# Gated DeltaNet and MoBA trunk on one core: the transposed 32x32 blocks of a merge from one VectorE transposition, not from TensorE products

## The chip, the core and the metric

The kernel runs on one core of a Trainium2 chip. The metric is the device time of one execution in microseconds (us); lower is better. Before the change three runs took 305.55, 305.79 and 303.6 us, the median is 305.55 us. One more execution was profiled. It took 301.56 us, of which 299.7 us lie between the first and the last instruction of the program.

## The reference, cut to what matters

A sequence of 256 positions of width 1024 goes through a gated-DeltaNet layer and then through a MoBA attention layer; each is followed by a layer norm over a weighted residual. All is float32. The change lies in the first layer, in the solution of small unit lower triangular systems:

```
def gated_delta_rule_chunked(q, k, v, g, beta):
    ...
    lower = jnp.where(strict, jnp.einsum('nbhid,nbhjd->nbhij', k_beta, k) * decay, 0.0)
    a_mat = jnp.eye(C, dtype=jnp.float32) + lower
    w = lax.linalg.triangular_solve(a_mat, k_beta * jnp.exp(gc)[..., None],
                                    left_side=True, lower=True, unit_diagonal=True)
    u = lax.linalg.triangular_solve(a_mat, v * beta[..., None],
                                    left_side=True, lower=True, unit_diagonal=True)
```

Around it stand projections of the input (q, k, v, z), a causal convolution of four taps, a read-out with an RMS norm and a gate, an output projection, and in the second layer the projections k, q, v, z, one 256-wide causal softmax attention for each of 8 heads, and an output projection.

## The kernel before, in words

Weights arrive as raw tiles of 128x1024, in the order in which they are used. ScalarE rounds each to a high part (`hi`), VectorE subtracts to get the low part (`lo`), and TensorE makes every projection as three products, high by high, high by low and low by high. A raw tile's place is free for the next load when its `lo` is written. Every instruction is recorded through small helpers, so that a profile gives nearly all of them one line (L220), and groups are told apart by tile names.

The kernel works with chunks of 128 positions, so that each of the 8 heads has two triangular 128x128 matrices, 16 in all. They are inverted in two groups of four heads, 8 matrices each, by `inverse(grp)`. VectorE or GpSimd inverts the 16x16 diagonal blocks. Then the blocks are merged: 16 to 32, 32 to 64, 64 to 128. The tile `TR` of a group holds its result `RR`, a working copy `TC` with two halves, half 0 with the inverses of the diagonal blocks and half 1 with the transposes of these, and `T64`. In the merge of 16 to 32, which the change touches, four 32x32 blocks lie in the four quarters of the partitions and 8 matrices side by side:

- `ps_x`: products of the matrix blocks (`ME`) by half 0 of `TC`; VectorE copies a part of the result under a mask into `XI` (COPY_PREDICATED).
- `ps_y`: products of half 1 of `TC` and `XI` in both orders, which give the 32x32 inverses and their transposes; ScalarE copies both from PSUM back into `TC` at once, 512 columns.
- VectorE copies diagonal blocks of `TC` into `RR` and `T64` (six copies, TR<-TR), and the merge of 32 to 64 begins: `ps_x5`, a ScalarE copy to `X`, `ps_y5`, then 64 to 128 with `ps_x6` and `ps_y6`. (The profile leaves the 5 and 6 out: x of 32x32 with 32 records and y<-TR,X are the second merge, 64x64 the third.)

A product of float32 operands shows as two records on TensorE in the trace, one of the rounded type or a transposition as one.

The group's result goes to `solve(grp)`: products `ps_s`, and for each chunk a read-out, `read_out`: products `ps_o`, ScalarE squares (`jk`), VectorE `rs`, a power on GpSimd, VectorE `og` (four instructions), TensorE transposition `ps_og`, ScalarE `o`, VectorE `o`. The first products of the output projection (`ps_y<-hi,o`) need both read-outs of group 0.

What sets the order of the instructions on each engine is a planner that runs while the kernel is written down. Projections are the spine of TensorE's queue; after each step of the spine the planner looks at a list of chains (the convolutions, `inverse`, `solve`, `read_out`, layer norms) by rank, and issues the next step of each whose operands it holds to be there by its own table of costs. The splits of weights into `hi` and `lo` are issued in the same way. So another instruction in one chain can move steps of the others in all queues. When the spine needs something that is not there, the planner lets TensorE's time run on until it is.

Of the kernel before, what the change touches and what calls it, by code (L numbers as in the profile page):

```python
# [307 lines left out]
def body(ctx, tc, x, xt, cst_in, w0, wp, a_ln_g, a_ln_b, b_ln_g, b_ln_b, out):  # L308
    ctx.enter_context(tc.manual_schedule())
    nc = Clock(tc.nc)  # L310
# [3 lines left out]
    def rot(pool, shape, dtype, tag, name, bufs):  # L314
        assert tag in ("raw", "hi", "lo") or free(tag)(), (tag, name)
        t = pool.tile(shape, dtype, tag=tag, name=name, bufs=bufs)
        nc.rotate(rings.setdefault(tag, [bufs]), t, bufs)
        return t

    def free(tag, n=1):  # L320

        def test():
            ring = rings.get(tag, [9])
            last = len(ring) - ring[0]
            return all(ring[i] in ended for i in range(max(1, last), max(1, last + n)))
        return test

    def end(*tiles):
        ended.update(getattr(t, "tensor", t).name for t in tiles)
# [13 lines left out]
    def bank(shape, name):  # L343
        return rot(psB, [P] + shape, F32, "b", name, NB)

    def acc(name):
        ring = rings.get("a", [9])
        old = ring[-NA] if len(ring) > NA else None
        pipe.wait(lambda: free("a")() and (old is None or nc.last[old] + 150 <= pipe.now() + 50))
        return rot(psA, [P, 512], F32, "a", name, NA)  # L350
# [168 lines left out]
    blocks = [slice(32 * b, 32 * b + 32) for b in range(4)]  # L519

    XI = [cst.tile([P, 8, 32], F32, name=f"XI{g}") for g in range(2)]
# [146 lines left out]
    def gs_head(h):  # L668
# [41 lines left out]
        if n_md[h // 4] == 4:  # L710
            pipe.add(inverse(h // 4), R_INV)
# [8 lines left out]
    def inverse(grp):  # L720
# [9 lines left out]
        TC = T[:, 1024:1536].rearrange("p (w q c) -> p w q c", w=2, q=8)  # L730
# [35 lines left out]
        ps = bank([8, 32], "ps_x")  # L766
# [4 lines left out]
        nc.vector.copy_predicated(XI[grp], m32.to_broadcast([P, 8, 32]), ps)  # L771
        end(ps)
        yield "t", [XI[grp], free("b")]
        ps = bank([2, 8, 32], "ps_y")
        for q in range(8):
            for b in blocks:
                nc.tensor.matmul(ps[b, 0, q, :], TC[b, 1, q, :], XI[grp][b, q, :], start=True, stop=True)
            for b in blocks:
                nc.tensor.matmul(ps[b, 1, q, :], XI[grp][b, q, :], TC[b, 1, q, :], start=True, stop=True)
        yield "a", [ps]  # L780
        nc.scalar.copy(TC, ps)
        end(ps)
        yield "t", [TC, free("b")]
        for b in blocks:
# [4 lines left out]
        ps = bank([8, 32], "ps_x5")  # L789
# [9 lines left out]
        ps = bank([2, 8, 32], "ps_y5")  # L799
# [12 lines left out]
        ps = bank([8, 64], "ps_x6")  # L812
# [7 lines left out]
        ps = bank([8, 64], "ps_y6")  # L820
# [205 lines left out]
    ps_y = {}  # L1026
# [186 lines left out]
    ps_y = {}  # L1213
# [14 lines left out]
    ps_y = [acc("ps_y2") for _ in range(2)]  # L1228
# [5 lines left out]
    ps_y = [acc("ps_y2"), acc("ps_y2")[:, 0:256], acc("ps_y2")[:, 0:256]]  # L1234
# [23 lines left out]
```

## Time and profile before

| what | value |
|---|---|
| median of three runs | 305.55 us (303.6 to 305.79) |
| the profiled execution, its span | 301.56 us, 299.7 us |
| TensorE products busy | 289.6 us, 97% of the span |
| VectorE busy | 210.8 us, 70% |
| ScalarE busy | 161.5 us, 54% |
| DMA, mean over the span | 165 GB/s |
| chain that ended last | TensorE 92%, no visible cause ("issue") 4%, VectorE 1%, ScalarE 1% |

The chain that ended last follows the work back from the last instruction to whatever released each step. Products are pipelined in TensorE, so the durations of single products overlap; what counts is the distance from start to start, or the length of a stretch of the chain. The merge of group 0 that the change touches runs from 99.6 to 107 us after the span's start, the one of group 1 from 126.5 to 136 us.

### The profile page before, as it was taken

To read this page: it belongs to the slowest core of one execution; us is meant where nothing else is said; L and a number is where in the kernel's file an instruction comes from. 1 tells how busy PE (TensorE), PEld (TensorE's weight loads), DVE (VectorE), ACT (ScalarE), POOL (GpSimd) and SP (SyncE) were. 2 spreads that over 40 slices of the span, in tenths; PEclk is the share of its full clock that TensorE was granted. 3 is DMA by queue.
4 is the path that set the end of the run, shared out by engine and by line. 5 is a ranking of instruction groups with operands and counts; after the bars stand their busy time and mean duration, and the time that the engine had idled before them with its cause. 6 is when DMAs were issued, how large, how long until landed. Compare 5 with 4: busy or idle time off the path is not lost.

```text
span 299.7 us, 6567 instructions
## 1 busy us (share of the span) xinstructions
PE 289.6 (97%) x2598; PEld 267.7 (89%) x2598; DVE 210.8 (70%) x477; ACT 161.5 (54%) x329; POOL 51.1 (17%) x92
## 2 busy tenths in 40 slices
PE   8999999999999999989999999999999999999990
PEld 7899998999999989978987888999999999998890
DVE  0799389999999586678339993865655655762545
ACT  2689986535776552845533525775555558561000
POOL 8003211348856100110020010000000000000101
PEclk9999999999999999999999999999999999999997
DMA  7996425569576702424449065785444447400012
GB/s 226 375 333 206 142 71 176 178 192 309 172 275 161 260 24 32 124 97 138 150 165 363 31 198 160 266 311 188 143 138 144 148 143 271 142 0 2 0 70 71
DMA packets 19934, 49.43 MB, mean 165 GB/s; under 512 B 6304, under 2 KB 7968, under 8 KB 19904
## 3 DMA queue, kind: packets, MB, share of 16 engines
q1 hardware_dynamic: 18592, 46.73, 47.8%
q0 software_dynamic: 448, 1.18, 1.4%
q10 hardware_dynamic: 864, 1.11, 1.1%
q8 instruction: 20, 0.33, 0.4%
q14 instruction: 10, 0.08, 0.1%
HBM read 46.65 MB, written 2.36 MB: 164 GB/s over the span
## 4 chain that ended last, share of the span: by engine, by line
PE 92%; issue 4%; DVE 1%; ACT 1%; POOL 0%; POOLq 0%; DVEq 0%; ACTq 0%
PE ps_kq L220 15%; PE ps_bkq L220 15%; PE ps_y L220 13%; PE ps_z L220 8%; PE ps_v L220 8%; PE ps_bv L220 7%; PE ps_bz L220 7%; PE ps_g L220 4%; PE ps_o L220 2%; PE ps_ot L220 2%; PE ps_sc L220 2%; PE ps_s L220 1%; PE ps_warm L220 1%; PE ps_x L220 1%; PE ps_gb L220 1%
## 5 line engine op out<-in xcount | busy, mean ns | idle before, releaser
L220 DVE TENSOR_TENSOR lo<-raw,hi 128x1024 fp32r<-128x1024 f32 (+1 forms) x79 | 95.5, 1217 | 10.4 <-ACT hi L220 10.0
L220 ACT CAST hi<-raw 128x1024 fp32r<-128x1024 f32 (+1 forms) x79 | 80.3, 1037 | 8.9 <-DMA raw<-in_wp_dram 4.3
L220 PE MATMUL ps_y<-hi,o 128*128 128x512 f32 (+1 forms) x144 | 43.1, 373 | 0.0
L220 PE MATMUL ps_bkq<-x1h,hi 128*128 128x256 f32 x128 | 37.9, 296 | 0.0
L220 PE MATMUL ps_kq<-xh,hi 128*128 128x256 f32 x128 | 36.9, 288 | 0.0
L220 PE MATMUL ps_kq<-xl,hi 128*128 128x256 f32 x128 | 35.9, 280 | 0.0
L220 PE MATMUL ps_kq<-xh,lo 128*128 128x256 f32 x128 | 35.9, 280 | 0.0
L220 PE MATMUL ps_bkq<-x1l,hi 128*128 128x256 f32 x128 | 35.5, 277 | 0.0
L220 PE MATMUL ps_bkq<-x1h,lo 128*128 128x256 f32 x128 | 35.5, 277 | 0.0
L220 PEld LDWEIGHTS ps_y<-hi,o 128*128 128x128 f32 x144 | 26.1, 189 | 4.3
L220 POOL TENSOR_TENSOR mv<-mv,nhalf 128x1 f32<-128x1 f32 x4 | 3.8, 951 | 133.3 <-DVE mv L220 133.3
L220 PE MATMUL ps_y<-lo,o 128*128 128x512 f32 (+1 forms) x72 | 26.3, 365 | 0.0
L220 DVE SCALAR_TENSOR_TENSOR cv<-ps_kq,cst_sb,cv 128x255 f32<-128x255 f32 (+2 forms) x48 | 21.6, 471 | 4.0 <-ACT cv L220 3.8
L220 PEld LDWEIGHTS ps_bkq<-x1l,hi 128*128 128x128 f32 x128 | 24.1, 188 | 0.2
L220 PEld LDWEIGHTS ps_kq<-xh,lo 128*128 128x128 f32 x128 | 24.3, 190 | 0.0
L220 PEld LDWEIGHTS ps_bkq<-x1h,hi 128*128 128x128 f32 x128 | 24.1, 188 | 0.2
L220 PEld LDWEIGHTS ps_kq<-xh,hi 128*128 128x128 f32 x128 | 24.2, 189 | 0.0
L220 PEld LDWEIGHTS ps_kq<-xl,hi 128*128 128x128 f32 x128 | 24.1, 188 | 0.0
L220 PEld LDWEIGHTS ps_bkq<-x1h,lo 128*128 128x128 f32 x128 | 24.1, 188 | 0.0
L220 PE MATMUL ps_v<-xh,hi 128*128 128x256 f32 x64 | 18.7, 292 | 0.0
L220 PE MATMUL ps_v<-xl,hi 128*128 128x256 f32 x64 | 17.9, 280 | 0.2 <-issue 0.2
L220 PE MATMUL ps_bz<-x1h,hi 128*128 128x256 f32 x64 | 18.1, 282 | 0.0
(177 smaller groups left out, 678.1 us busy)
## 6 DMA issues: line engine op xcount, KB each, us to landing
raw<-in_wp_dram SPq DMA_DIRECT2D x77, 512.0 KB, 4.0
md<-ME POOLq DMA_DIRECT2D x8, 128.0 KB, 2.3
late<-in_x_dram SPq DMA_DIRECT2D x1, 1024.0 KB, 5.0
zraw<-in_w_dram ACTq DMA_DIRECT2D x4, 136.0 KB, 4.3
zraw<-in_w_dram ACTq DMA_DIRECT2D x2, 272.0 KB, 5.0
x_sb<-in_xt_dram SPq DMA_DIRECT2D x4, 128.0 KB, 4.0
x_sb<-in_xt_dram SPq DMA_DIRECT2D x2, 256.0 KB, 4.9
raw<-in_wp_dram SPq DMA_DIRECT2D x2, 256.0 KB, 4.4
```

Source lines behind the costliest of these rows:

```text
L220: r = f(*args, **kw)
```

## The change: what it does, and the diff

The products of `ps_y` that gave the transposed results are left out, 32 for each group, 64 in all. `ps_y` has 256 columns instead of 512. ScalarE copies them into half 0 of `TC`. A single VectorE instruction reads the same PSUM tile, transposes each 32x32 block by itself, and writes half 1 of `TC`.

```diff
@@ -771,14 +771,13 @@
         nc.vector.copy_predicated(XI[grp], m32.to_broadcast([P, 8, 32]), ps)
         end(ps)
         yield "t", [XI[grp], free("b")]
-        ps = bank([2, 8, 32], "ps_y")
+        ps = bank([8, 32], "ps_y")
         for q in range(8):
             for b in blocks:
-                nc.tensor.matmul(ps[b, 0, q, :], TC[b, 1, q, :], XI[grp][b, q, :], start=True, stop=True)
-            for b in blocks:
-                nc.tensor.matmul(ps[b, 1, q, :], XI[grp][b, q, :], TC[b, 1, q, :], start=True, stop=True)
+                nc.tensor.matmul(ps[b, q, :], TC[b, 1, q, :], XI[grp][b, q, :], start=True, stop=True)
         yield "a", [ps]
-        nc.scalar.copy(TC, ps)
+        nc.scalar.copy(TC[:, 0], ps)
+        nc.vector.transpose(TC[:, 1].rearrange("p q c -> p (q c)"), ps.rearrange("p q c -> p (q c)"))
         end(ps)
         yield "t", [TC, free("b")]
         for b in blocks:
```

The planner then moves other steps. Up to `ps_y` of group 0 the queues are the same. The largest move is around the merge of group 1 (its tiles are TR_1361 and XI_149) and the read-outs of group 0. On VectorE, before, from the second `rs` of group 0 on:

```order
L220 SCALAR_TENSOR_TENSOR rs<-sso,eq 128x4
L220 COPY_PREDICATED XI_149<-m_145,ps_x 128x256
L220 SCALAR_TENSOR_TENSOR cv<-ps_v,cst_sb,cv 128x255
L220 TENSOR_TENSOR lo_1707<-raw_1394,hi_1706 128x1024
L220 SCALAR_TENSOR_TENSOR og<-ps_o,rs,zs 128x128 x4
L220 SCALAR_TENSOR_TENSOR cv<-ps_v,cst_sb,cv 128x254
L220 COPY TR_1361<-TR_1361 32x8x32 x6
L220 SCALAR_TENSOR_TENSOR o_1772<-ps_og,nnw,o_1772 128x4x128
L220 COPY TR_1361<-ps_y_2083 32x8x32 x2
```

And in the changed kernel, from the masked copy on:

```order
L220 COPY_PREDICATED XI_149<-m_145,ps_x 128x256
L220 SCALAR_TENSOR_TENSOR cv<-ps_v,cst_sb,cv 128x253
L220 TENSOR_TENSOR lo_1830<-raw_1413,hi_1829 128x1024
L220 SCALAR_TENSOR_TENSOR o_1742<-ps_og,nnw,o_1742 128x4x128
L220 STREAM_TRANSPOSE TR_1361<-ps_y 128x256
L220 SCALAR_TENSOR_TENSOR rs<-sso,eq 128x4
L220 TENSOR_TENSOR lo_1923<-raw_1772,hi_1922 128x1024
L220 COPY TR_1361<-TR_1361 32x8x32 x6
L220 SCALAR_TENSOR_TENSOR og<-ps_o,rs,zs 128x128 x4
L220 COPY TR_1361<-ps_y_2037 32x8x32 x2
L220 TENSOR_TENSOR lo_2030<-raw_1811,hi_2029 128x1024
L220 SCALAR_TENSOR_TENSOR o_1742<-ps_og,nnw,o_1742 128x4x128
```

The second read-out (`rs`, `og`, the last `o`) has moved behind the masked copy and the transposition, the six copies stand ahead of `og` instead of behind it, and two more `lo` stand ahead of the last `o`.

On TensorE, before, where group 1's merge begins:

```order
L220 MATMUL ps_og<-ident,og 128x128 x4
L220 MATMUL ps_o<-Z,ME 128x128 x8
L220 MATMUL ps_x<-TR_1361,ME 32x32 x32
L220 MATMUL ps_vt<-ident,cv 128x128 x2
L220 MATMUL ps_z<-hi_1319,xh 128x256
L220 MATMUL ps_z<-lo_1320,xh 128x256
L220 MATMUL ps_z<-hi_1319,xl 128x256
```

And in the changed kernel:

```order
L220 MATMUL ps_x<-TR_1361,ME 32x32 x32
L220 MATMUL ps_og<-ident,og 128x128 x4
L220 MATMUL ps_z<-hi_1319,xh 128x256
L220 MATMUL ps_z<-lo_1320,xh 128x256
L220 MATMUL ps_z<-hi_1319,xl 128x256
L220 MATMUL ps_o<-Z,ME 128x128 x8
L220 MATMUL ps_y<-XI_149,TR_1361 32x32 x32
```

The products `ps_o` of the second read-out, and the transposition `ps_og` of the first, now come after `ps_x` of the merge; 36 products of `ps_z` stand between the end of `ps_v` and `ps_x`, where there were 21.

On TensorE, before, up to the first product of the output projection:

```order
L220 MATMUL ps_y_2083<-TR_1361,X_2072 32x32 x2
L220 MATMUL ps_z<-hi_1319,xh 128x256
L220 MATMUL ps_z<-lo_1320,xh 128x256
L220 MATMUL ps_z<-hi_1319,xl 128x256
L220 MATMUL ps_z<-hi_1319,xh 128x256
L220 MATMUL ps_z<-lo_1320,xh 128x256
L220 MATMUL ps_z<-hi_1319,xl 128x256
L220 MATMUL ps_y<-hi_1373,o_1772 128x512
```

And in the changed kernel:

```order
L220 MATMUL ps_y_2037<-X_2022,TR_1361 32x32
L220 MATMUL ps_y_2037<-TR_1361,X_2022 32x32 x2
L220 MATMUL ps_og<-ident,og 128x128 x4
L220 MATMUL ps_x_2079<-TR_1361,ME 64x64 x8
L220 MATMUL ps_y<-hi_1373,o_1742 128x512
L220 MATMUL ps_y<-lo_1374,o_1742 128x512
```

The last `ps_z` now stands ahead of `ps_y5`, three products after `ps_x5`; the second `ps_og` and `ps_x6` stand ahead of the first product of the output projection, where 6 products of `ps_z` stood.

## Rows read from the trace of the kernel before

**Rows 1.** The page: busy us, share of the span, instructions, by engine.
```profile
PE 289.6 (97%) x2598; PEld 267.7 (89%) x2598; DVE 210.8 (70%) x477; ACT 161.5 (54%) x329; POOL 51.1 (17%) x92
```
**Rows 2.** The page: the chain that ended last, by engine.
```profile
PE 92%; issue 4%; DVE 1%; ACT 1%; POOL 0%; POOLq 0%; DVEq 0%; ACTq 0%
```
**Rows 3.** Waits of TensorE products: total us, times, longest.
```profile
PE ps_y L220 <- issue: 1.2, 2, 0.9
PE ps_warm L220 <- DVE ones L220: 1.1, 1, 1.1
PE ps_vt L220 <- ACT cv L220: 0.2, 1, 0.2
PE ps_v L220 <- issue: 0.2, 1, 0.2
```
**Rows 4.** Chain in order of time: start, length, work, records.
```profile
105.33 0.22 issue
...
124.73 1.80 PE ps_o L220 x16
...
126.62 1.15 ACT jk L220 x8
...
129.26 0.90 issue
...
134.37 0.33 issue
...
136.70 1.07 PE ps_x L220 x16
```
**Rows 5.** Busy us and records of each engine in stretches of TensorE's queue.
```profile
101.52:102.73 1.21, 1.21 (x129) 1.17 (x128) 1.00 (x1) 0.69 (x1) 0.00 (x0) 1.00 0.33 125
...
130.15:134.35 4.20, 4.20 (x128) 3.76 (x128) 2.79 (x11) 2.00 (x4) 0.00 (x0) 1.00 0.39 131
```
**Rows 6.** DMA queues: packets, MB.
```profile
q8 instruction: 20, 0.33, 0.4%
```
**Rows 7.** Timeline of TensorE: start, us from first start to last end, records.
```profile
126.45 0.75 PE L220 MATMUL ps_x<-TR,ME 32*32 32x32 f32 x64
127.14 0.44 PE L220 MATMUL ps_vt<-ident,cv 128*128 128x128 f32 x2
127.33 0.36 PE L220 MATMUL ps_z<-hi,xh 128*128 128x256 f32 x1
127.53 0.28 PE L220 MATMUL ps_z<-lo,xh 128*128 128x256 f32 x1
127.65 0.28 PE L220 MATMUL ps_z<-hi,xl 128*128 128x256 f32 x1
...
131.96 0.69 PE L220 MATMUL ps_x<-TR,ME 32*32 32x32 f32 x32
132.58 0.66 PE L220 MATMUL ps_og<-ident,og 128*128 128x128 f32 x4
132.99 0.36 PE L220 MATMUL ps_z<-hi,xh 128*128 128x256 f32 x1
...
135.85 0.39 PE L220 MATMUL ps_y<-hi,o 128*128 128x512 f32 x1
```
**Rows 8.** Timeline of VectorE, the same columns, idle time before.
```profile
127.80 0.16 DVE L220 SCALAR_TENSOR_TENSOR rs<-sso,eq 128x4 f32<-128x4 f32 x1 [1.19 <-ACT jk L220]
127.88 0.44 DVE L220 COPY_PREDICATED XI<-m,ps_x 128x256 f32<-128x256 uint8 x1
128.21 0.47 DVE L220 SCALAR_TENSOR_TENSOR cv<-ps_v,cst_sb,cv 128x255 f32<-128x255 f32 x1
128.60 1.21 DVE L220 TENSOR_TENSOR lo<-raw,hi 128x1024 fp32r<-128x1024 f32 x1
129.73 1.12 DVE L220 SCALAR_TENSOR_TENSOR og<-ps_o,rs,zs 128x128 f32<-128x128 f32 x4
130.77 0.47 DVE L220 SCALAR_TENSOR_TENSOR cv<-ps_v,cst_sb,cv 128x254 f32<-128x254 f32 x1
131.48 1.62 DVE L220 COPY TR<-TR 32x256 f32<-32x256 f32 x6 [0.24 <-ACT TR L220]
134.20 0.75 DVE L220 SCALAR_TENSOR_TENSOR o<-ps_og,nnw,o 128x512 fp32r<-128x512 f32 x1 [1.10 <-ACT o L220]
135.15 0.87 DVE L220 COPY TR<-ps_y 32x256 f32<-32x256 f32 x2 [0.20 <-PE ps_y L220]
```
**Rows 9.** VectorE groups by shape: busy us, mean ns.
```profile
L220 DVE TENSOR_TENSOR lo<-raw,hi 128x1024 fp32r<-128x1024 f32 x77 | 94.2, 1230 | 10.2 <-ACT hi L220 9.7
...
L220 DVE COPY late<-ps_ot 128x256 f32<-128x256 f32 x8 | 3.4, 424 | 7.2 <-PE ps_ot L220 7.2
...
L220 DVE COPY TR<-TR 32x256 f32<-32x256 f32 x12 | 3.1, 281 | 0.4 <-ACT TR L220 0.2
```
**Rows 10.** Timeline of ScalarE: copies out of the merges.
```profile
102.89 0.59 ACT L220 COPY TR<-ps_y 128x512 f32<-128x512 f32 x1 [0.69 <-issue]
...
108.41 0.36 ACT L220 COPY TR<-ps_y 32x256 f32<-32x256 f32 x1 [1.51 <-DVE TR L220]
...
132.70 0.75 ACT L220 COPY X<-ps_x 32x256 f32<-32x256 f32 x2 [1.25 <-PE ps_x L220]
```

## The prediction

> **What bounds the kernel now.** First the page's busy shares: TensorE has 97% of the span, VectorE 70%, ScalarE 54% [rows 1]. Since busy products overlap, the chain that ended last comes next: 92% of it is TensorE [rows 2]. Then its waits: after the start, products waited four times, 0.2 us for ScalarE and 1.45 us in three gaps with no visible cause [rows 3, 4]. So a microsecond taken from TensorE's queue is a microsecond of the time, as long as nothing new makes that queue wait. All three gaps lie in the stretch with the small products of the merges.
>
> The gaps have a pattern. From the restart after the gap of 129.26 (at 130.15) to the next gap TensorE ran exactly 128 products and 128 weight loads, 256 instructions [rows 5]. A DMA queue for instructions moved 20 packets, 0.33 MB [rows 6]; 2598 products and as many loads are 20.3 times 256 [rows 1]. I read this as code arriving in blocks of 256 instructions, and TensorE running out of it where 128 products pass fast. The Trainium skill says otherwise in part (Runtime: NRT & Kernel Launch, Instruction fetch mechanics): it gives the same blocks of 256, but holds that fetching them is mostly hidden. By that rule the gaps have another cause and nothing done to the number of products removes them; the rows agree on the block and speak against the hiding.
>
> **The work that goes.** `ps_y` of group 0 has 64 products, 128 records, and took 1.21 us from start to the product behind it [rows 5]. Half of it goes: 0.61 us, and 0.61 us again in group 1, together 1.22 us on the engine that bounds.
>
> ScalarE's copy shrinks from 512 columns, 0.59 us, to 256, which I take at 0.36 us, a copy of as many columns [rows 10]. The profile shows no transposition on VectorE. The row nearest to it copies the same 128x256 float32 from PSUM to SBUF: 0.42 us [rows 9], which I take. Ends of the range: 0.28 us, a 256-column copy within SBUF, and 1.23 us, an instruction of four times the columns [rows 9], should eight blocks need several passes; no row makes it likelier than the plain copy.
>
> **Group 0.** Nothing waits for these 0.42 us: the products that read half 1 are `ps_y5`, and between stand 21 `ps_v`, which I take at the 0.12 us of a `ps_z` (127.53 to 127.65 [rows 7]), and `ps_x5` at 0.63 us (131.96 to 132.58 [rows 7]), 3.1 us. So 0.61 us is gained. The gap of 0.22 us at 105.33 should go too. Its block now holds 19 records of `ps_y`, 29 `ps_v`, `ps_x5` and `ps_y5`, some 4.9 us, while the block of 130.15 had its code after 4.20 us and a gap of 0.33 us [rows 4, 5]. TensorE is 0.83 us early after it.
>
> **Group 1: where it is given back.** I follow the new order with the old durations, start to start.
>
> TensorE before began `ps_x` of group 1 at 126.45 [rows 7]. In the new order `ps_og` (0.41 us, from 132.58 to 132.99 [rows 7]) and `ps_o` (1.80 us [rows 4]) come behind it instead, and 15 products of `ps_z` at 0.12 us, 1.8 us, and one pair `ps_vt`, 0.2 us [rows 7], come ahead. 126.45 - 0.83 - 2.21 + 2.0 = 125.4. Then `ps_x` 0.69 to 126.1, `ps_og` to 126.5, three `ps_z` to 126.85, `ps_o` to 128.65, `ps_y` 0.61 to 129.26.
>
> VectorE takes the masked copy at 126.2, then by the distances of [rows 8]: copy 0.33, cv 0.39, `lo` 1.13, `o` 0.75, to 128.8. The transposition has to wait for `ps_y`, to 129.36, and ends at 129.8. `rs` waits for the squares, 1.15 us behind `ps_o` [rows 4]: it is done at 130.0. From there VectorE has no gap: `lo` 1.13, six copies 1.62, `og` 1.04, two copies 0.87, `lo` 1.13, `o` 0.75. The sum is 6.54 us, so the last `o` is there at 136.5 and the output projection can start at 136.6.
>
> TensorE meanwhile has too little to do: six `ps_z` 0.9, `ps_vt` 0.2, `ps_x5` 0.63, three `ps_z`, to 131.5. The copies to `X` take 0.75 us after `ps_x5` [rows 10], so `ps_y5` runs from 132.0 to 132.65 (0.5 us idle, where six `ps_z` and `ps_og` covered it before). `og` is written at 133.8, so TensorE waits 1.2 us for it, then 0.5 us for `T64` and 0.75 us for `o`. About 2.9 us idle in all, where there were gaps of 0.90 and 0.33 us [rows 4]. The block of code that begins with this `ps_y` ends within `ps_y5`; a gap there as long as the longest, 0.90 us, would be over before `og` is written, so I count none on top.
>
> Before, the output projection started at 135.85 [rows 7], but with `ps_x6` (1.07 us [rows 4]) and a pair `ps_vt` (0.2) still to do, which now are done by then. Like for like that is 137.1. So the change comes out at 136.6 - 137.1 = -0.5 us: of 0.83 + 0.61 us and two gaps, together 2.67 us, some 2.2 us are given back as waits for VectorE. Behind this point the queue has the same products, `lo` is two tiles ahead of what it was, and TensorE had no wait before; I expect none.
>
> **The sum.** 301.56 - 0.5 = 301.1 us against the profiled execution. The median of the runs stands 4.0 us higher than that execution; taken off the median it is 305.0 us.
>
> **The rivals.**
>
> The whole gain arrives. The planner's move costs nothing, because VectorE reaches the last `o` in time (`og` overlaps more than I count, or `ps_z` covers the waits). Then 1.22 us of products and 1.45 us of gaps go: 302.9 us. For it: the planner found this order by its own costs, and before the change its order left only one short wait on ScalarE in the whole kernel [rows 3]. Against it: VectorE's queue from the transposition on, as counted. Chance 0.2.
>
> The products go and the gaps stay. A block of code is then as late as before, wherever it ends. Only 1.22 us are gained: 304.3 us. This is what the hiding in the Trainium skill's page on the runtime would leave, since the gaps would not come from code. Chance 0.1.
>
> Slower than before. VectorE becomes the bound of this stretch by more than I count. From the transposition to the last `o` it has no gap, so what the transposition takes beyond 0.42 us goes one for one to the start of the output projection. The point from which it decides is 0.42 + 0.5 = 0.9 us. At the upper bound of 1.23 us the projection starts 0.8 us later, which is 0.3 us slower than before, 305.85 us; a `lo` more ahead of it (1.13 us), held up by its weights, makes it 307.0 us. For it: 70% of VectorE is busy, and in this stretch all of it. Against it: a plain copy of that shape takes 0.42 us. Chance 0.15.
>
> That the change does not do what it says can be left aside: the new order has 32 products of `ps_y` in each group instead of 64, and one transposition each.
>
> **The numbers.** The forecast, 305.0 us, has 0.55, with -1.2 to +0.5 us around it for my hand count of waits. All cases lie between 302.9 and 307.0 us. The three runs shown differ by 2.2 us, and the profiled execution lies below all of them, so a median may fall half a microsecond beyond the lower end: 302.4 to 307.0 us. About 1%, 3 us, is what a measurement of this kernel can tell from no change. Only the whole gain, -0.9%, comes near that: faster by more than 1% gets 0.09, mostly a part of that rival's 0.2. Slower by more than 1% gets 0.05, since even the bounds of the third rival together stay at half of it. Within 1%: 0.86.
>
> **What would show it.** In the profile after: `ps_y` of the first merge with 64 records in about 0.61 us, twice; a transposition of about 0.4 us; no gap of "issue" at 105 us; the waits of TensorE between 131 and 137 us with VectorE's `og`, `TR` and `o` as what ended them, some 2.9 us in sum instead of 1.2; the first product of the output projection near 136.6 us. If those waits are missing, the first rival is right. If the gaps with no cause are as long as before, the second. If the transposition takes over 0.9 us, the third. I am wrong altogether if the queue behind 140 us shows waits that were not there.

## The result, and the profile after

The changed kernel takes 305.65 us (median of 20 runs, 304.32 to 307.29), the kernel before, on the same chips, 303.5 us (20 runs, 301.6 to 306.31). The ratio is 1.008, with a 95% interval of 1.0061 to 1.010: about 2.4 us slower. (Here and below, a run over 1.5% above the fastest of its kernel is left out of a ratio, so that a ratio is not always the quotient of the medians.) The forecast was a gain of 0.5 us. The sign was wrong. That the time lies only 0.65 us above the forecast of 305.0 us is luck: the forecast was counted from the first three runs of the kernel before, whose median of 305.55 us stands 2 us above that of all 20. The profiled execution took 305.25 us, 303.2 of them span, where before it was 301.56 and 299.7.

The page of the changed kernel: busy us by engine, the granted clock of TensorE in 40 slices, the instruction queue, the chain by engine.

```profile
PE 293.1 (97%) x2470; PEld 270.2 (89%) x2470; DVE 211.5 (70%) x479; ACT 161.5 (53%) x329; POOL 52.6 (17%) x92
...
PEclk9999999999999999995999999999999999999998
...
q8 instruction: 19, 0.31, 0.4%
...
PE 88%; issue 3%; DVE 3%; DMA 2%; ACT 2%; POOL 0%; POOLq 0%; DVEq 0%
```

TensorE has 128 products and 128 weight loads fewer on record and is busy 3.5 us *longer* [rows 1]. The 5 in the row of the clock is the first reason; another, in the second layer, comes at the end. Its waits, as in [rows 3]: the gaps of 1.45 us with no visible cause are gone, and one wait for VectorE has come.

```profile
PE ps_og L220 <- DVE og L220: 1.2, 1, 1.2
PE ps_warm L220 <- DVE ones L220: 1.1, 1, 1.1
PE ps_vt L220 <- ACT cv L220: 0.2, 1, 0.2
```

The merge of group 0 ran with no gap, as forecast. The chain there (start, length, work), where `ps_y` took 1.21 us before [rows 5]:

```profile
102.31 0.68 PE ps_y L220 x50
102.99 1.24 PE ps_v L220 x9
104.24 0.62 PE ps_x L220 x32
```

VectorE from the last step ahead of the transposition to the last `o`, to be held against [rows 8]:

```profile
128.55 0.74 DVE L220 SCALAR_TENSOR_TENSOR o<-ps_og,nnw,o 128x512 fp32r<-128x512 f32 x1
131.21 0.45 DVE L220 STREAM_TRANSPOSE TR<-ps_y 128x256 f32<-128x256 f32 x1 [1.92 <-ACT TR L220]
131.58 0.12 DVE L220 SCALAR_TENSOR_TENSOR rs<-sso,eq 128x4 f32<-128x4 f32 x1
131.62 1.21 DVE L220 TENSOR_TENSOR lo<-raw,hi 128x1024 fp32r<-128x1024 f32 x1
132.75 1.58 DVE L220 COPY TR<-TR 32x256 f32<-32x256 f32 x6
134.37 1.13 DVE L220 SCALAR_TENSOR_TENSOR og<-ps_o,rs,zs 128x128 f32<-128x128 f32 x4
...
138.41 0.75 DVE L220 SCALAR_TENSOR_TENSOR o<-ps_og,nnw,o 128x512 fp32r<-128x512 f32 x1 [0.76 <-ACT o L220]
```

The transposition takes 0.45 us, but VectorE stood still for 1.92 us ahead of it, and not for `ps_y`: it waited for ScalarE's copy out of the same `ps_y`. ScalarE's queue shows what that copy stood behind, a convolution step and the squares:

```profile
130.23 0.29 ACT L220 ACTIVATE jk<-ps_o 128x128 f32<-128x128 f32 x1
...
130.48 0.43 ACT L220 ACTIVATE cv<-cv 128x256 f32<-128x256 f32 x1
130.79 0.39 ACT L220 COPY TR<-ps_y 128x256 f32<-128x256 f32 x1
```

TensorE behind it, beside [rows 7]:

```profile
134.78 1.10 PE L220 MATMUL ps_og<-ident,og 128*128 128x128 f32 x4 [1.19 <-DVE og L220]
136.00 1.55 PE L220 MATMUL ps_x<-TR,ME 64*64 64x64 f32 x16
137.48 0.79 PE L220 MATMUL ps_y<-hi,o 128*128 128x512 f32 x1
```

The first product of the output projection starts at 137.48, before the last `o` is begun at 138.41: it needs the other read-out's `o`, so the wait for the last `o` that I had counted does not exist.

Now two stretches of 2 us after another (stretch, us, then busy us and records of TensorE, weight loads, VectorE, ScalarE, GpSimd, then granted clock, DMA share, GB/s), first of the kernel before, then of the changed one.

```profile
132.00:134.00 2.00, 2.00 (x54) 1.83 (x56) 1.04 (x4) 1.25 (x3) 0.00 (x0) 1.00 0.32 125
134.00:136.00 2.00, 1.67 (x55) 1.52 (x53) 1.57 (x3) 0.16 (x1) 0.00 (x0) 1.00 0.03 8
136.00:138.00 2.00, 2.00 (x21) 1.53 (x20) 1.97 (x4) 1.88 (x4) 0.00 (x0) 1.00 0.00 0
```

```profile
132.00:134.00 2.00, 1.45 (x53) 1.09 (x51) 1.97 (x6) 1.93 (x5) 1.78 (x1) 1.00 0.24 27
134.00:136.00 2.00, 1.10 (x5) 0.56 (x5) 1.89 (x8) 0.19 (x1) 0.00 (x0) 1.00 0.66 229
136.00:138.00 2.00, 2.00 (x17) 1.86 (x18) 1.62 (x2) 1.51 (x3) 0.00 (x0) 0.63 0.04 14
138.00:140.00 2.00, 2.00 (x12) 1.27 (x11) 1.59 (x2) 0.95 (x2) 0.00 (x0) 0.50 0.61 219
```

TensorE lacks 1.45 us of work between 132 and 136 us, and then its granted clock falls to 0.50, that is from 2.4 to 1.2 GHz, from 136.5 to 143.35 us. A queue full of products that runs 6.83 us at half speed loses up to 3.4 us. Before, the clock is 1.00 through all of this.

The bill, by matching TensorE's products of the two profiles one by one: where both queues are still alike, at 100 us, the changed kernel is 0.72 us late, a difference at the start. At 160 us, from where both queues are alike to the end, it is 2.3 us late. So between them the change cost 1.6 us. A last 1.1 us come after 255 us, where each of the last 250 products takes about 4.5 ns longer; that is taken up at the end. The clock's part in this is not the whole 3.4 us: the experiment with idle products below prices it at 1.9 us, so that all the rest of the change *gained* 0.3 us.

### The profile page after: what moved, and what is told of

Its sections match the earlier page's. It is cut to its first block, busy times and chain, and to the rows that moved or that the text cites. A ratio compares the mean times of both kernels' runs of the same rounds, so it can differ in the third digit from the quotient of the medians.

```text
span 303.2 us, 6322 instructions
## 1 busy us (share of the span) xinstructions
PE 293.1 (97%) x2470; PEld 270.2 (89%) x2470; DVE 211.5 (70%) x479; ACT 161.5 (53%) x329; POOL 52.6 (17%) x92
## 4 chain that ended last, share of the span: by engine, by line
PE 88%; issue 3%; DVE 3%; DMA 2%; ACT 2%; POOL 0%; POOLq 0%; DVEq 0%
PE ps_kq L220 15%; PE ps_bkq L220 15%; PE ps_y L220 13%; PE ps_v L220 8%; PE ps_bz L220 7%; PE ps_bv L220 7%; PE ps_z L220 7%; PE ps_g L220 4%; DMA raw<-in_wp_dram 2%; PE ps_ot L220 2%; PE ps_sc L220 2%; PE ps_s L220 1%; PE ps_warm L220 1%; PE ps_x L220 1%; PE ps_gb L220 1%
## 5 line engine op out<-in xcount | busy, mean ns | idle before, releaser
L220 PE MATMUL ps_y<-hi,o 128*128 128x512 f32 (+1 forms) x144 | 44.5, 384 | 0.0
L220 PEld LDWEIGHTS ps_y<-hi,o 128*128 128x128 f32 x144 | 26.8, 194 | 4.9
L220 PE MATMUL ps_y<-lo,o 128*128 128x512 f32 (+1 forms) x72 | 27.2, 378 | 0.0
L220 PE MATMUL ps_bz<-x1h,lo 128*128 128x256 f32 x64 | 17.9, 280 | 0.0
```

The source lines that it names most:

```text
L220: r = f(*args, **kw)
```

## The experiments

**My theory** was that the transposition itself is worth its 2.7 us, and that the new order, with a transposition that waits for ScalarE, leaves TensorE without work and takes its clock. **Rivals**: the transposition costs what it gains; the clock is a by-product that costs nothing; the order alone is to blame.

**The change with the old order.** The planner is told the costs of the 32 products that are gone and of the longer copy; all queues keep the old order. (The helper's line is L238 there, and the new instructions have lines of their own.)

```diff
+        nc.as_before(ps, TC, XI[grp])       # books 32 products on TensorE
         yield "a", [ps]
-        nc.scalar.copy(TC[:, 0], ps)
-        nc.vector.transpose(TC[:, 1]..., ps...)
+        tc.nc.scalar.copy(TC[:, 0], ps)     # issued past the planner
+        tc.nc.vector.transpose(TC[:, 1]..., ps...)
+        nc.copied_as_before(ps, TC)         # books the copy of 512 columns
```

> The change with the order of the kernel before: the planner is told the old costs, so that the queues hold the old order, with 32 products of ps_y in each group left out and one transposition put in. Theory (the new order is what costs, by TensorE's waits and the fall of its clock after them): faster than before by 1.2 to 2.7 us, ratio 0.991 to 0.996, the granted clock at 1.00 between 130 and 145 us. Rival (the transposition itself costs, by VectorE's time and its wait for ScalarE's copy): slower than before as the changed kernel is, ratio 1.005 to 1.010.

Measured: 300.28 us, ratio 0.9898 (0.986 to 0.9936). The theory holds, with a little more gain than its bracket had, and the first rival falls: the same instructions in the old order gain 3.1 us. Its one profiled execution shows that the clock can fall here too. There `ps_y5` of group 0 waited for a transposition that stood behind VectorE steps whose DMA was late; the clock fell behind that wait too (0.50 for 10.24 us from 108.5), and that execution took 304.65 us:

```profile
PE ps_y L238 <- DVE TR L799: 1.5, 1, 1.5
```

**The new order with the old products.** The kernel before, all 64 products and the copy of 512 columns, with the planner's bookings of the changed kernel.

```diff
-                nc.tensor.matmul(ps[b, 1, q, :], XI[grp][b, q, :], TC[b, 1, q, :], ...)
+                tc.nc.tensor.matmul(ps[b, 1, q, :], XI[grp][b, q, :], TC[b, 1, q, :], ...)
-        nc.scalar.copy(TC, ps)
+        tc.nc.scalar.copy(TC, ps)
+        nc.as_changed("Activation", ps, TC[:, 0], 80 + 0.833 * 256)
+        nc.as_changed("DVE", ps, TC[:, 1], 68 + 1.042 * 256)
```

> The kernel before with the order of the changed one: all 64 products of ps_y and the 512-column copy stay, no transposition, but the planner is told the costs of the change. Theory (the order costs): slower than before by the 2.4 us that the changed kernel lost and about 1 us for the products that it saved, ratio 1.008 to 1.013, with waits for VectorE's og and TR between 131 and 137 us and the clock at 0.5 behind them. Rival (the transposition costs): ratio 0.998 to 1.002.

Measured: 304.63 us, 1.0031 (0.9998 to 1.0065). A miss. The order alone costs 0.3%, if anything. Nine of its twelve runs had a mean clock of 0.986 and more; in the profiled one, with 0.985, it fell (0.50 for 6.83 us from 138.3). Its 64 extra products take 1.2 us of TensorE's queue, and nothing waits for a transposition. So the order by itself is not the whole loss.

**Idle products in the hole.** The changed kernel with nine 128x128 products that nobody reads, five ahead of the second `ps_og` and four ahead of `ps_x6`.

```diff
+        for _ in range(0 if grp == 0 else 4):            # ahead of ps_x6
+            tc.nc.tensor.matmul(ps...[:, 0:P], ident, ident, start=True, stop=True)
...
+        for _ in range(5 if (grp, t) == (0, 1) else 0):  # ahead of ps_og
+            tc.nc.tensor.matmul(ps[:, 0, :], ident, ident, start=True, stop=True)
```

> The changed kernel, same order, with nine idle products of 128x128 float32 on TensorE, five ahead of the second ps_og and four ahead of ps_x6 of group 1, where it waits for VectorE; their results are overwritten. They take about 2 us of a wait that is there anyway. Theory (3.4 us of the loss is the clock at half for 6.8 us, which the waits bring on): the clock stays at 1.00, ratio to the kernel before 0.995 to 0.999. Rival (the waits alone cost, the clock hurts nothing since VectorE bounds there): ratio 1.006 to 1.010 as without them, whatever the clock shows.

Measured: 302.25 us, 0.9961 (0.9937 to 0.9985). More work makes the kernel 1.2% faster than the change without it, and faster than before. All 12 runs have a mean clock of 0.991 to 0.997; the 20 of the changed kernel have 0.975 to 0.984. (A mean of 0.991 does not exclude a short fall: the last experiment's profile has it with 3.41 us at 0.50.) The same stretches as above:

```profile
132.00:134.00 2.00, 1.86 (x56) 1.57 (x56) 1.96 (x7) 1.95 (x4) 1.62 (x1) 1.00 0.19 43
134.00:136.00 2.00, 2.00 (x15) 1.57 (x14) 1.91 (x7) 0.03 (x1) 0.00 (x0) 1.00 0.71 227
...
138.00:140.00 2.00, 1.71 (x20) 1.21 (x18) 1.75 (x2) 0.79 (x2) 0.00 (x0) 1.00 0.72 240
```

The products fill the hole, the clock stays at 1.00, and `ps_x6` starts 0.5 us *later* than in the changed kernel. The last products of the merge (`ps_y6`, which need ScalarE's copy to `X`) start at nearly the same time in both. First the changed kernel, then this one, which is 0.16 us early from 100 us on:

```profile
139.06 1.97 PE L220 MATMUL ps_y<-TR,X 64*64 64x64 f32 x16
```

```profile
138.87 1.14 PE L220 MATMUL ps_y<-TR,X 64*64 64x64 f32 x16 [0.29 <-ACT X L220]
```

So up to `ps_y6` the slow clock had cost nothing: it only took up a wait for `X`, and so far the rival is right. Behind it the two queues are the same product by product, and only the clock differs. At 160 us the kernel with idle products is 0.23 us behind the kernel before, where it was 0.56 us behind at 100 us: it gained 0.3 us, and the changed kernel lost 1.6 us. That the fall of the clock turned a gain of 0.3 us into this loss is shown; its price is 1.9 us, not the 3.4 us of my expectation. The spans differ by 3.2 us, but 1.1 us of that are the slower last 250 products, which this profile does not have.

**The transposition ahead of the copy.** The two instructions are exchanged in the program, nothing else.

```diff
-        nc.scalar.copy(TC[:, 0], ps)
         nc.vector.transpose(TC[:, 1].rearrange("p q c -> p (q c)"), ps.rearrange("p q c -> p (q c)"))
+        nc.scalar.copy(TC[:, 0], ps)
```

> The changed kernel, same order on every engine, with the transposition written down ahead of ScalarE's copy, so that it waits for TensorE alone and the copy waits for it. Theory (order and waits): in group 1 the transposition starts about 1.2 us earlier, og and T64 come about 1 us earlier, TensorE waits some 1 us less; if the clock still falls the ratio to before is 1.004 to 1.006, if it does not 0.994 to 0.998. Rival (VectorE's wait for the copy is the whole cause): ratio at most 0.998 with no waits for VectorE left.

Measured: 303.99 us, 1.0008 (0.9977 to 1.004). VectorE and TensorE in its profile:

```profile
129.83 0.45 DVE L220 STREAM_TRANSPOSE TR<-ps_y 128x256 f32<-128x256 f32 x1 [0.80 <-PE ps_y L220]
...
133.21 1.12 DVE L220 SCALAR_TENSOR_TENSOR og<-ps_o,rs,zs 128x128 f32<-128x128 f32 x4
```

```profile
133.61 1.10 PE L220 MATMUL ps_og<-ident,og 128*128 128x128 f32 x4 [0.29 <-DVE og L220]
...
137.87 1.14 PE L220 MATMUL ps_y<-TR,X 64*64 64x64 f32 x16 [1.00 <-ACT X L220]
```

Now the transposition waits for `ps_y` alone and starts 1.4 us earlier, and the wait for `og` shrinks from 1.19 to 0.29 us. So the wait for ScalarE came from the order in which the program wrote the two instructions. They read one PSUM tile and write two halves of one SBUF tile; which of the two tiles tied them, no run separates. Part of the gap has moved to a wait of 1.00 us for `X`, and the clock fell in most of the runs: three with a mean of 0.995 took 301.94 to 302.12 us, four with 0.980 to 0.984 took 302.23 to 304.15, five with 0.974 and 0.975 took 304.5 to 305.66. The profiled run is one of the first three. Its stretches lack 1.55 us of work, as much as those of the changed kernel but spread over 6 us, and its clock stays:

```profile
132.00:134.00 2.00, 1.57 (x53) 1.09 (x51) 1.93 (x9) 1.87 (x4) 0.62 (x1) 1.00 0.61 190
134.00:136.00 2.00, 1.88 (x20) 1.38 (x20) 1.91 (x5) 0.68 (x2) 0.00 (x0) 1.00 0.21 80
136.00:138.00 2.00, 1.00 (x5) 0.52 (x6) 1.24 (x3) 1.79 (x3) 0.00 (x0) 1.00 0.20 37
```

**The old order and the transposition ahead of the copy.** The first experiment, with the transposition issued right behind the products.

```diff
+        tc.nc.vector.transpose(TC[:, 1]..., ps...)
         yield "a", [ps]
         tc.nc.scalar.copy(TC[:, 0], ps)
-        tc.nc.vector.transpose(TC[:, 1]..., ps...)
```

> The change with the order of the kernel before, and the transposition recorded right behind the products of ps_y, ahead of ScalarE's copy. In the old order with the transposition at the copy's place it stood behind ten steps of the other group's inversion, which wait for a DMA, and ps_y5 of group 0 waited 1.5 us for it. Theory (TensorE's waits and the fall of its clock are all that can cost here): that wait goes, the clock stays at 1.00 up to the end, ratio to before 0.986 to 0.992. Rival (the products saved are worth 1.2 us at most and the rest of the gain of the kernel with the old order is chance): 0.995 to 0.997.

Measured: 300.05 us (299.35 to 300.17), 0.9905 (0.9875 to 0.9935). It is faster than both kernels, with a clock of 0.992 or more in all six runs. In its profile the gain between 100 and 160 us is 2.6 us, matched product by product as above; the whole gain of my first rival was 2.67. Its one new wait between 100 and 160 us and one of the stretches:

```profile
PE ps_x L238 <- ACT TR L799: 0.3, 1, 0.3
```

```profile
132.00:134.00 2.00, 2.00 (x29) 1.56 (x20) 1.91 (x4) 0.31 (x2) 0.00 (x0) 1.00 0.04 8
```

**A stall in the kernel before, short and long.** Six, then twelve idle products on VectorE ahead of the second `og`; nothing of the change is in these kernels.

```diff
         og = rot(tmp, [P, 4, P], F32, "og", "og", 2)
+        for _ in range(6 if (grp, t) == (0, 1) else 0):   # 12 in the second
+            tc.nc.vector.tensor_mul(junk, ones2, ones2)
```

> The kernel before, nothing of the change, with six idle VectorE products of 128x256, about 2.4 us, ahead of the second og of group 0, where VectorE had some 1 us of slack. Theory (waits for VectorE there bring the clock down, whoever makes them): TensorE waits about 2 us between 131 and 139 us, then the clock shows 0.5 for 6.8 us in most runs, mean clock 0.975 to 0.985, ratio 1.008 to 1.018. Rival (a wait costs its own length and the fall of the clock in the changed kernel has to do with its fewer products): mean clock 0.990 to 0.997, ratio 1.003 to 1.007.

Six: 303.06 us, 1.0003 (0.9973 to 1.0034), a miss of both sides. They took 2.71 us, and no wait of TensorE for `og` shows in the profile: in the old order VectorE has that much slack ahead of `og`, where products of `ps_z` still cover.

> The kernel before, with its order and its 64 products, and twelve idle products of 128x256 on VectorE (5.4 us) ahead of the second `og`; nothing of the change is in it. Six of them cost nothing (1.0003), because TensorE hardly waited. Theory (waits of TensorE of some 2.5 us before the output projection, whatever causes them, take the clock down): TensorE now waits 2.5 to 3.5 us for `og`, about 1 us of which the work behind it takes back; the granted clock shows 0.50 for 6 to 10 us behind 138 us in the profile, and the time is 5 to 7 us longer: 1.016 to 1.023. Rival (the clock falls for another reason, such as the new order or the transposition, and a wait costs only itself): the clock stays at 1.00 and only the wait is paid: 1.006 to 1.012.

Twelve: 306.69 us in four runs, 1.018 (1.0101 to 1.0259). The wait on TensorE, and the stretches around it:

```profile
PE ps_og L220 <- DVE og L220: 2.2, 1, 2.2
```

```profile
134.00:136.00 2.00, 0.86 (x4) 0.50 (x5) 1.97 (x7) 0.00 (x0) 0.00 (x0) 1.00 0.00 0
136.00:138.00 2.00, 2.00 (x56) 1.80 (x56) 1.89 (x8) 0.69 (x1) 0.00 (x0) 0.72 0.03 8
138.00:140.00 2.00, 2.00 (x8) 1.90 (x9) 1.91 (x5) 0.45 (x2) 0.00 (x0) 0.50 0.00 0
```

So the clock falls to 0.50 with the old products and the old order too, behind waits alone. They are more than the one that I put in: the gap with no visible cause inside `ps_y` of group 1 is 1.52 us in this profile, where it was 0.90, and TensorE lacks 3.75 us of work between 128 and 136 us. The clock stayed at 0.50 for 3.41 us, less than the 6 to 10 that I had expected, so I had the effect and not its length. The ratio is in the theory's bracket, but its interval reaches into the rival's; the rows of the clock decide.

**One group at a time.** The new code `if grp == 0`, or `if grp == 1`, and the old code otherwise.

> The change in group 0 alone; group 1 keeps its 64 products. The planner moves the second read-out behind the merge of group 1 as in the changed kernel. Theory (the new order costs, and it comes from group 0): waits for og and T64 between 131 and 138 us and the clock down in most runs, ratio 1.001 to 1.006, since group 1's products fill 0.6 us and no transposition stands in VectorE's queue there. Rival (the transposition in group 1 costs): 0.995 to 0.998.

Group 0 alone, which brings most of the new order: 301.5 us, 0.9952 (0.9921 to 0.9984). A miss: better than the theory said. Its profiled run lost the clock (0.50 for 10.24 us from 136.5, 305.79 us), nine of the other eleven had 0.986 or more.

> The change in group 1 alone; the order stays that of the kernel before but for two low parts. Theory (the new order costs): 0.61 us of products and part of the gaps of 0.90 and 0.33 us go, clock at 1.00, ratio 0.993 to 0.998. Rival (the transposition in group 1 and its wait for ScalarE's copy cost): 1.003 to 1.008.

Group 1 alone, with the read-outs in their old places (on TensorE some `ps_z`, and the second `ps_og`, moved): 301.88 us, 0.9973 (0.9941 to 1.0005), in the theory's bracket. Group 0 alone gains 0.5%, group 1 alone 0.3% if anything, and both together lose 0.8%. So the loss needs both halves: the new order of the read-outs and the transposition of group 1 in it. That it is the transposition's wait for ScalarE that matters there is not shown: in the profile of group 1 alone the transposition did not wait at all, and with the two instructions exchanged it waited for `ps_y` alone, and the clock fell in most of the runs all the same.

**Code blocks shifted.** The kernel before, with one warming product replaced by 32 small ones at its start: 62 more records, the order behind them unchanged.

```diff
-    keep_warm(WARM)
+    keep_warm(WARM - 1)
+    for i in range(32):
+        k = slice(32 * (i % 4), 32 * (i % 4) + 32)
+        tc.nc.tensor.matmul(ps_warm[k, 0:32], ones[k, 0:32], ones[k, 0:32], start=True, stop=True)
```

> The kernel before, with one of the warming products at its start replaced by 32 products of 32x32 (62 more records on TensorE, some 0.3 us, long before the merges); the queue behind is the same. Theory (the gaps with no cause are code that comes in blocks of 256 instructions): every block boundary comes 62 records earlier in the program, so the gaps move: the one of 0.22 us from `ps_v` back into `ps_y` of group 0, the one of 0.90 us from `ps_y` of group 1 back to the products `ps_o` or `ps_z` ahead of it, where records pass slowly, and shrinks or goes; the one of 0.33 us likewise. Rival (the gaps belong to their places in the program, such as reads and writes of PSUM): they stay behind `ps_y` of group 0, within `ps_y` of group 1 and ahead of `ps_y5`, with some 0.2, 0.9 and 0.3 us.

One execution, 305.29 us. Its waits, and its chain at the two gaps:

```profile
PE ps_y L220 <- issue: 3.1, 1, 3.1
...
PE ps_x L220 <- issue: 0.7, 1, 0.7
```

```profile
102.64 3.08 issue
...
135.40 0.73 issue
```

The gap that stood behind `ps_v` at 105.33 now cuts `ps_y` of group 0 in two; the one of 0.33 us now cuts `ps_x5`; the one of 0.90 us is gone. Counted in records from the start, the first and the last stand where they stood, behind the 983rd and the 1491st, with other instructions there. The 1363rd is among the same small products of `ps_y` as before, but the 128 records up to it now took 6.6 us, with slower products among them, where they took 2.4 us; no gap is left there. So the gaps belong to the count of instructions and not to a place in the program. Whether one shows and how long it is does not follow from the count: 0.22 us became 3.08, and 0.90 became nothing. Behind the gap of 3.08 us the clock fell as well, to 0.50 for 3.41 us from 106.7. That blocks come every 256 instructions is what the Trainium skill states (Runtime: NRT & Kernel Launch, Instruction fetch mechanics); that crossing one is mostly hidden does not always hold here, where small products pass at 9.5 ns a record (1.21 us for 128 [rows 5]): the gaps were 0.22 to 3.08 us.

## Why the prediction was wrong

- **Products and gaps**: right. `ps_y` went to 0.68 us in each group (0.61 forecast), and the gaps of 1.45 us went. The second rival had them stay; it falls. The first, the whole gain, came only in the old order.
- **The prices**: right. The transposition took 0.45 us against 0.42, ScalarE's copy 0.39 against 0.36 [rows 10]. The third rival had the sign that came, by a mechanism that didn't: the transposition never neared 0.9 us.
- **The order of VectorE's queue and the wait for `og`**: right in size, 1.19 us against 1.2. The start of it failed: "the transposition has to wait for `ps_y`, to 129.36" - it waited for ScalarE's copy and started at 131.21. I had read the diff as two independent instructions. Two errors cancel: `og` began some 0.9 us later than I had it (beyond the 0.72 us of the start), but `ps_og` needs only the first of its four instructions (134.37 to 134.78) and not all of them, 1.04 us.
- **The waits of 2.9 us**: 0.75 us too many. Some 0.3 us within `ps_y5`, 1.19 us ahead of `ps_og`, and 0.8 us from there to `ps_x6` (1.22 us from start to start, where `ps_og` takes 0.41 [rows 7]) make 2.3 us, against 2.2 forecast for these three. (By the busy time the hole is 1.45 us, since the four products of `ps_og`, each waiting for its part of `og`, count as busy.) "0.75 us for `o`" was no wait: the first products need only the part of `o` that the other read-out wrote. I took the tile for one piece.
- **What decided was in none of my terms.** "Behind this point the queue has the same products ... I expect none" is the step that failed: I summed waits as if each cost only its own length, and put what comes behind them at nothing. Behind the hole TensorE ran 6.83 us at 1.2 GHz, and that cost 1.9 us, which turns a gain of 0.3 us into a loss of 1.6. There was a wait behind this point too, for `X` ahead of `ps_y6` (0.29 us with idle products in the hole). Without the clock the like-for-like count stands at -0.3 us where I had -0.5, so the sum of what I did count was nearly right, in part by errors that cancel. Both rows of [rows 5] show a granted clock of 1.00, and I never asked what would keep it there.
- The new order alone is not the whole loss, as my expectation for it had it: with the old products it cost 0.3%, with an interval that reaches 1.

## What to carry to other kernels

Where a change takes work from an engine that is nearly always busy, ask not only how long the new holes are but what TensorE's granted clock does behind them: here a hole of 1.45 us cost 1.9 us again, and nine useless products in it paid for themselves. Price a slow clock only where TensorE has nothing else to wait for: the part of it that fell ahead of the wait for `X` was free. Where two engines take their input from the same PSUM tile, write the instruction that others wait for first; here the second was held behind the first. And when a planner reorders after a small saving, try the saving in the old order: it held the whole gain, 1%, here.

## What the runs showed of the hardware

- In the changed kernel the clock falls behind a hole in which no single wait is longer than 1.2 us. Where it fell ahead of the end of the program, it stayed at 0.50 for 3.41, 6.83 or 10.24 us in the profiles here. The same kernel can meet it in some runs and not in others (exchanged instructions: 301.94 and 305.66 us).
- How much work is missing does not decide it alone: behind 1.55 us between 132 and 138 us the clock stayed (exchanged instructions), behind 1.12 us between 130 and 138 us it fell (the new order with the old products). What else decides stays open.
- The gaps at block boundaries vary from 0.2 to 3.1 us, at the same count of instructions; in the profile with twelve idle VectorE products the first and the last of the three are not there.
- In three of the twelve profiles (the changed kernel, the new order with the old products, the exchanged instructions) each product from about 255 us on takes some 4.5 ns longer, 117.8 against 113.3 ns from start to start in the second layer's projection, at a granted clock of 1.00. Over 250 products this is 1.1 us. All three have the new order, but so has the kernel with the idle products, which shows 113.3. Whether it belongs to a kernel or to a run, and what causes it, stays open.
